# A four-layer decoder step on one core: layer norm's sum of squares by three plain additions in place of two strided sums

## The chip, the core and the metric

The kernel runs on one core of a Trainium2 chip. The metric is the device time of one execution in microseconds (us). A core has five engines that run their own instruction streams in order and wait for each other by semaphores: PE (TensorE, matrix products; its weight loads are listed as PEld), DVE (VectorE), ACT (ScalarE), POOL (GpSimd) and SP (SyncE, which here only issues DMAs).

## The reference, cut to what matters

One inference step of a decoder trunk of four layers, in float32, for a prompt of 512 positions and 8 single sample tokens: 520 columns of 1024 features. Each layer is a token mixer (sparse attention, gMLP, HGRN2, sparse attention) and a SwiGLU feed-forward block, and behind each of the eight stands a residual with a layer norm; gMLP has one more norm inside.

```python
def layer_norm(x, g, b):
    mu = jnp.mean(x, axis=-1, keepdims=True)
    var = jnp.mean(jnp.square(x - mu), axis=-1, keepdims=True)
    return (x - mu) * lax.rsqrt(var + LN_EPS) * g + b

def deepnorm(x, h, g, b):
    return layer_norm(DEEPNORM_ALPHA * x + h, g, b)
```

So nine layer norms run in a step, each over 1024 features of 520 columns.

## The kernel before, in words

Activations lie feature-major: eight blocks of 128 features, one feature a partition, and along the free axis the 520 columns, treated as two halves of 256 and 264 (`HS`, L18). A float32 matrix product is made of three products of split parts (L248 to L250), for each of the 128-row blocks k of a unit; a unit is one 128-column block of weights. After every second k, `mm` calls `tick` (L251, L252), so a tick comes after each six matmuls. A tick takes one step of every generator that has been spawned (L221 to L231): this is how work of DVE, ACT and POOL, and PE's few other products, are put between the matmuls. The instructions stand in each engine's stream in the order in which the program issues them. Weights arrive by DMA on SP's queue (L87) and are split by ACT and DVE (L100, L101) two units ahead.

`out_proj` (L364) adds the last product of a layer's block to x (L381 or L383), POOL adds up the column sums (L360, L362; the last block on DVE), and when feature block 7 of a half is there, it spawns `ln` for that half (L387). The seven last blocks run by halves: all of half 0, then all of half 1. So half 0's norm runs beside half 1's matmuls, and half 1's norm beside the first units of the next phase, which read half 0 only. gMLP spawns the same `ln` at L465.

`ln` (L263) has these steps, one a tick: three ticks of nothing (`WM`); the mean, a product of the column sums with a matrix of 1/1024 (L277, on PE); two steps that each subtract the mean from two pairs of feature blocks (L284, DVE, 512 or 528 columns) and square them (L285, ACT); two steps that each sum four squared blocks to one row (L293, DVE, a reduction that reads its 1024 or 1056 elements with the block index innermost); then the variance, the product of the two rows with the same matrix (L298, on PE, two products into one PSUM bank); the inverse root (Ln and Exp on ACT, L339 and L341; a Newton step on DVE, L348 to L352); and the scaling and split by pairs (L306 to L317, L271). `WV`, the ticks ahead of the variance, is 0. The float32 products L277 and L298 appear in the trace as two matmul records each.

With `direct` (half 1 of the very last norm alone) there are no reductions: the eight squared blocks go to PE as eight products. Squared blocks lie in tiles of the large pool `g` (38 tiles), the summed rows in the pool `row` (8 tiles).

The lines that the change touches:

```python
            nc.scalar.activation(sq[-1][:, 2 * (j % 2):2 * (j % 2) + 2], xs, AF.Square)
            if j % 2:
                yield
        for j in range(2):
            if direct:
                q += [sq[j][:, i] for i in range(4)]
            else:
                q.append(self.row()[:, :n])
                nc.vector.tensor_reduce(q[-1], sq[j].rearrange("p b t -> p t b"), op=OP.add, axis=AX.X)
            yield
        yield from wait(WV)
        pv = self.ps()
        for i, r in enumerate(q):
            nc.tensor.matmul(pv[:, :n], self.ones, r, start=i == 0, stop=i == len(q) - 1)
```

Of the kernel before, what the change touches and what calls it, by code (L numbers as in the profile page):

```python
# [11 lines left out]
OP = mybir.AluOpType  # L12
AX = mybir.AxisListType
# [6 lines left out]
EPS = 1e-5  # L20
CH = (8, 7, 7)
NFF = sum(CH)
SLOTS = 38        # tiles of the pool that nearly everything lives in
WM, WV = 3, 0     # layer norm: ticks before the mean's and the variance's matrix products
# HGRN: order of a head's four projections (q, forget gate, v, output gate), units that run by halves first, ticks
# before a head's levels, levels built ahead, ticks of the sample's part, rate of the last head, output units beside it
HORD, HF, HW, BUILD, SW0, SWAIT, HRATE, EARLY = (0, 1, 2, 3), 6, 1, 3, 0, 8, 2, 6
# NSA: units between scores and mix, blocks between transposes and values, steps that exp and the like are put off
LAG, PVLAG, DEFER = 2, 3, 1
# NSA: steps a tick of attention (beside W_in, beside W_out) and of compression, and of the others for one of attention  # L30
RATE, RATE2, CRATE, STEPS = 4, 4, 1, 1
# NSA: steps that the sample's pages, values and compressed rows are waited for, tokens whose pages load ahead
CWAIT, EWAIT, AHEAD = 8, 5, 5
# [8 lines left out]
def alternate(*gs):  # L42
    """Steps of some generators in turn, until all end."""
    live = list(gs)
    while live:
        for x in list(live):
            try:
                next(x)
                yield
            except StopIteration:  # L50
                live.remove(x)
# [17 lines left out]
class Weights:  # L69
    """Streams weight blocks: DMA, then a split in two float32r parts, ahead of their use."""  # L70

# [45 lines left out]
class Split:  # L117
    """Activations by blocks of features, as two float32r parts whose sum is exact."""

# [24 lines left out]
class Net:  # L144
# [67 lines left out]
    def spawn(self, g, rate=1.0):  # L212
        """A generator whose steps are issued between those of the matrix products."""
        self.par.append([g, rate, 0.0])
        return g
# [21 lines left out]
    def mm(self, unit, nk, R, half, ks=None, p=None):  # L237
        """One 128-column block of weights times the columns of a half: three passes a block of rows."""
        nc = self.nc
        H, L = self.W.need(unit)  # L240
        c0, c1 = HS[half]
        n = c1 - c0
        if p is None:
            p = self.ps()
        for k in ks or range(nk):
            s = slice(k * 128, k * 128 + 128)
            a, b = R.get(k, c0, c1)
            nc.tensor.matmul(p[:, :n], H[:, s], a, start=k == 0, stop=False)  # L248
            nc.tensor.matmul(p[:, :n], L[:, s], a, start=False, stop=False)  # L249
            nc.tensor.matmul(p[:, :n], H[:, s], b, start=False, stop=k == nk - 1)  # L250
            if k % 2:  # L251
                self.tick()  # L252
        return p

    @staticmethod
    def order(n, first, last):
        """(index, half): the first and the last few by halves, the others both halves together."""
        o = [(i, 0) for i in range(first)] + [(i, 1) for i in range(first)]
        for i in range(first, n - last):
            o += [(i, 0), (i, 1)]  # L260
        return o + [(i, 0) for i in range(n - last, n)] + [(i, 1) for i in range(n - last, n)]

    def ln(self, cols, li, sums, pair, X=None, out=None, direct=False):  # L263
        """Layer norm over the features, in place; its split goes to X, or out(j, c0, c1, pair) follows each pair.
        With direct, the tensor engine alone sums the squares."""
        nc = self.nc
# [6 lines left out]
        c0, c1 = cols  # L273
# [6 lines left out]
        for j in range(4):  # L280
# [5 lines left out]
            if j % 2:  # L286
                yield
        for j in range(2):
            if direct:
                q += [sq[j][:, i] for i in range(4)]  # L290
            else:
                q.append(self.row()[:, :n])
                nc.vector.tensor_reduce(q[-1], sq[j].rearrange("p b t -> p t b"), op=OP.add, axis=AX.X)  # L293
            yield
# [32 lines left out]
    def table(self, i):  # L327
        """The set of ScalarE's tables that the next functions need: one set for exp and ln together."""
        nc = self.nc
        if self.tab != i:  # L330
            self.tab = i
            nc.scalar.add_instruction(mybir.InstLoadActFuncSet(
                act_func_set_id=i, name=nc.get_next_instruction_name(), engine=mybir.EngineType.Activation))

    def guess(self, ys, vs):
        """y = exp(-ln(var + EPS) / 2), guesses at 1 / sqrt(var + EPS)."""
        self.table(LN_EXP)
        for y, v in zip(ys, vs):
            self.nc.scalar.activation(y, v, AF.Ln, bias=self.eps[:, 0:1])  # L339
        for y in ys:  # L340
            self.nc.scalar.activation(y, y, AF.Exp, scale=-0.5)  # L341

    def newton(self, ys, vs):
        """A Newton step from the guesses, and -2 times the results."""
        nc = self.nc
        ws = [self.row()[:, :y.shape[1]] for y in ys]
        for w, y, v in zip(ws, ys, vs):
            nc.vector.scalar_tensor_tensor(w, v, EPS, y, op0=OP.add, op1=OP.mult)  # L348
        for w, y in zip(ws, ys):
            nc.vector.tensor_mul(w, w, y)  # L350
        for w, y in zip(ws, ys):
            nc.vector.scalar_tensor_tensor(y, w, -3.0, y, op0=OP.add, op1=OP.mult)  # L352
# [11 lines left out]
    def out_proj(self, units, nk, R, scale, li, first=0, last=7, final=False, early=0):  # L364
        """x = scale * x + W h by blocks of features; with li the layer norm runs behind it."""
        nc = self.nc
# [153 lines left out]
    def bounds(self):  # L520
        """The heads' lower bounds of the forget gates, and the norm's gain."""
        nc, a = self.nc, self.a
# [23 lines left out]
    def hgrn(self, layer, plan):  # L546
# [26 lines left out]
        def sample(h, QK, FV, G, S0):  # L573
            """The sample tokens of a head: their states one step on, and what they read from them."""
            yield from wait(SW0)
# [27 lines left out]
        def head(h, QK, FV, G, smp):  # L603
# [6 lines left out]
            def build(i):  # L610
                """Queries times decays from a block's start, keys times decays to its end, by doubling blocks."""
                x, y = self.slot(), cur[i - 1]
# [22 lines left out]
            def odd(ap, i):  # L635
                """Columns in the second halves of the blocks of a level: its queries."""
                if i == 0:
                    return ap.rearrange("p c (n w) -> p c n w", n=1)
                return ap.rearrange("p c (n b w) -> p c n b w", b=2, w=2 ** (i - 1))[:, :, :, 1]
# [125 lines left out]
    def nsa(self, layer, plan):  # L765
# [49 lines left out]
        def summaries(cm, n, b):  # L815
            """Compressed keys and values of n pages; with b == 8, of the prompt, whose last page is the position term."""
            cv = cm.rearrange("p n (v l j) -> p n v l j", v=2, l=8)
# [15 lines left out]
        def compress():  # L833
            """Of the prompt first, then of each token's pages."""
            yield from wait(12)
# [46 lines left out]
        def attend():  # L882
            """Causal attention of the groups' heads over the prompt: three branches, by blocks of queries."""
            D, pv, due = {}, [], []
# [105 lines left out]
            def products(lag):  # L990
                """Values times transposed probabilities, behind the transposes."""
                while len(pv) > lag:
# [39 lines left out]
        def sample():  # L1032
            """Attention of the sample tokens, rows (token, head), over their pages, windows and new rows."""
            Qp = self.slot()[:, 0, :512].rearrange("p (v b c) -> p v b c", v=2, b=8)
# [22 lines left out]
            def rows(br, v):  # L1057
                """The keys or the values of each token's pages or window, loaded ahead."""
                ts = []
# [236 lines left out]
def constants(np):  # L1296
    """Arrays that depend on shapes alone: identity, masks, selectors."""
    p = np.arange(128)
# [12 lines left out]
def arrange(np, i):  # L1311
    """Inputs as the kernel reads them: permuted, with weights in blocks of 128 columns."""
    i = {k: np.asarray(v) for k, v in i.items()}
# [53 lines left out]
def results(r):  # L1367
    """Outputs as the reference has them."""
    y = r["yT"].transpose(2, 1, 0).reshape(T, 1024)
# [25 lines left out]
```

## Time and profile before

| what | us | share of the span |
|---|---|---|
| runs, median of 3 (lowest, highest) | 3125.0 (3124.13, 3129.43) | |
| profiled execution, span | 3127.9 | |
| PE busy | 2960.0 | 95% |
| PE weight loads busy | 2772.8 | 89% |
| DVE busy | 1734.5 | 55% |
| ACT busy | 1296.0 | 41% |
| POOL busy | 472.8 | 15% |

The profile is of one execution; its span lies within the runs' own spread, 2.9 us above their median. Busy time counts instructions as they run, so an engine can be far from busy and still be what another waits for. In a timeline row the first number is the start, the second the time from the start of the first to the end of the last of the merged instructions, and the bracket is the idle time of that engine ahead of it, with what ended it.

### The profile page before, as it was taken

To read this page: it belongs to the slowest core of one execution; us is meant where nothing else is said; L and a number is where in the kernel's file an instruction comes from. 1 tells how busy PE (TensorE), PEld (TensorE's weight loads), DVE (VectorE), ACT (ScalarE), POOL (GpSimd) and SP (SyncE) were. 2 spreads that over 40 slices of the span, in tenths; PEclk is the share of its full clock that TensorE was granted. 3 is DMA by queue.
4 is the path that set the end of the run, shared out by engine and by line. 5 is a ranking of instruction groups with operands and counts; after the bars stand their busy time and mean duration, and the time that the engine had idled before them with its cause. 6 is when DMAs were issued, how large, how long until landed. Compare 5 with 4: busy or idle time off the path is not lost. (4 is left out here: it accounts for less than half of the span.)

```text
span 3127.9 us, 56300 instructions
## 1 busy us (share of the span) xinstructions
PE 2960.0 (95%) x22730; PEld 2772.8 (89%) x22730; DVE 1734.5 (55%) x3821; ACT 1296.0 (41%) x2902; POOL 472.8 (15%) x446
## 2 busy tenths in 40 slices
PE   8898999999989999999899999999899999999997
PEld 8887468999988999998899889999888865799997
DVE  4887545333456633337777773333668866543334
ACT  4666434322345431234455443223456655332322
POOL 0222032000030300004222130000312212300002
PEclk9999999999999999999999999999999999999999
DMA  4222433223222222322222222232122143323221
GB/s 170 74 61 84 135 108 102 88 84 107 82 82 95 67 90 92 98 86 78 76 83 76 71 95 88 92 104 82 68 79 66 60 150 91 132 83 100 89 83 40
DMA packets 136039, 280.61 MB, mean 90 GB/s; under 512 B 13026, under 2 KB 76002, under 8 KB 135778
## 3 DMA queue, kind: packets, MB, share of 16 engines
q1 hardware_dynamic: 127168, 261.86, 26.6%
q10 hardware_dynamic: 7458, 10.95, 1.0%
q0 software_dynamic: 1152, 4.19, 0.5%
q8 instruction: 179, 2.93, 0.4%
q14 instruction: 82, 0.67, 0.1%
HBM read 263.69 MB, written 13.27 MB: 89 GB/s over the span
## 5 line engine op out<-in xcount | busy, mean ns | idle before, releaser
L248 PE MATMUL ps<-g 128*128 128x256 f32 (+1 forms) x6176 | 1784.2, 289 | 14.5 <-ACT g L100 13.2
L249 PE MATMUL ps<-g 128*128 128x256 f32 (+1 forms) x6176 | 1755.4, 284 | 6.8 <-DVE g L101 6.8
L250 PE MATMUL ps<-g 128*128 128x256 f32 (+1 forms) x6176 | 1757.1, 285 | 4.4 <-DVE g L271 2.7
L248 PEld LDWEIGHTS ps<-g 128*128 128x128 f32 x6176 | 1177.7, 191 | 37.9 <-ACT g L100 15.0
L249 PEld LDWEIGHTS ps<-g 128*128 128x128 f32 x6176 | 1177.3, 191 | 13.1 <-DVE g L101 8.3
L250 PEld LDWEIGHTS ps<-g 128*128 128x128 f32 x6176 | 1175.1, 190 | 6.1 <-DVE g L271 3.5
L101 DVE TENSOR_TENSOR g<-g 128x512 fp32r<-128x512 f32 (+1 forms) x708 | 468.6, 713 | 59.8 <-ACT g L100 52.5
L100 ACT CAST g<-g 128x512 fp32r<-128x512 f32 (+1 forms) x788 | 426.6, 608 | 118.9 <-DVE g L101 98.0
L419 DVE TENSOR_TENSOR row<-row,ps 128x256 f32<-128x256 f32 (+1 forms) x176 | 74.8, 425 | 515.7 <-PE ps L250 515.7
L209 ACT CAST g<-row 128x256 fp32r<-128x256 f32 (+1 forms) x192 | 78.6, 410 | 503.2 <-DVE row L419 491.6
L360 POOL TENSOR_TENSOR row<-x 128x256 f32<-128x256 f32 (+1 forms) x16 | 13.0, 812 | 1451.7 <-DVE x L383 1331.5
L418 ACT ACTIVATE row<-ps 128x256 f32<-128x256 f32 (+1 forms) x176 | 67.6, 384 | 334.3 <-PE ps L250 334.0
L951 ACT ACTIVATE g<-g,nst 128x128 f32<-128x128 f32 (+3 forms) x256 | 143.1, 559 | 109.8 <-DVE nst L949 109.3
L381 DVE SCALAR_TENSOR_TENSOR x<-x,ps 128x256 f32<-128x256 f32 (+1 forms) x128 | 52.9, 423 | 167.9 <-PE ps L250 167.8
L963 POOL TENSOR_SCALAR g<-g,nst 128x128 f32<-128x128 f32 (+3 forms) x64 | 76.5, 1195 | 442.7 <-DVE nst L956 378.7
L998 PE MATMUL ps<-g 128*128 128x512 f32 x384 | 141.4, 451 | 0.0
L949 DVE CUSTOM_DVE_ANT_0 g<-ps,ncst 128x128 f32<-128x128 f32 (+3 forms) x256 | 119.1, 482 | 39.4 <-PE ps L947 34.1
L947 PE MATMUL ps<-g 128*128 128x256 f32 (+2 forms) x512 | 123.9, 343 | 11.3 <-DVE nst L949 5.9
L985 ACT CAST g<-ps 128x512 fp32r<-128x512 f32 x160 | 91.9, 583 | 102.2 <-PE ps L982 83.2
L101 POOL TENSOR_TENSOR g<-g 128x512 fp32r<-128x512 f32 x80 | 105.0, 1333 | 172.8 <-ACT g L100 170.1
L383 DVE TENSOR_TENSOR x<-x,ps 128x256 f32<-128x256 f32 (+1 forms) x128 | 53.8, 424 | 135.5 <-PE ps L250 135.4
L210 DVE TENSOR_TENSOR g<-row,g 128x256 fp32r<-128x256 f32 (+1 forms) x192 | 81.7, 429 | 83.8 <-ACT g L209 83.8
(239 smaller groups left out, 2954.2 us busy)
## 6 DMA issues: line engine op xcount, KB each, us to landing
g<-ffn_in SPq DMA_DIRECT2D x176, 512.0 KB, 3.6
g<-ffn_out SPq DMA_DIRECT2D x64, 448.0 KB, 3.3
g<-nsa_in SPq DMA_DIRECT2D x42, 512.0 KB, 3.8
cm<-cache_cmp SPq DMA_DIRECT2D x64, 256.0 KB, 3.8
g<-cache_slc SPq DMA_DIRECT2D x128, 128.0 KB, 2.6
g<-cache_win SPq DMA_DIRECT2D x32, 512.0 KB, 6.5
g<-ffn_out SPq DMA_DIRECT2D x32, 512.0 KB, 3.5
g<-hgrn_in SPq DMA_DIRECT2D x32, 512.0 KB, 3.9
```

What stands on the lines that cost most here:

```text
L100: self.nc.scalar.copy(h[:, a:b], r[:, a:b])
L101: (self.sub[a > 0] or self.nc.vector).tensor_sub(l[:, a:b], r[:, a:b], h[:, a:b].bitcast(FT))
L209: self.nc.scalar.copy(h, src)
L210: self.nc.vector.tensor_sub(l, src, h.bitcast(FT))
L248: nc.tensor.matmul(p[:, :n], H[:, s], a, start=k == 0, stop=False)
L249: nc.tensor.matmul(p[:, :n], L[:, s], a, start=False, stop=False)
L250: nc.tensor.matmul(p[:, :n], H[:, s], b, start=False, stop=k == nk - 1)
L947: nc.tensor.matmul(p[:, :nn], q, kt[:, s, :nn], start=s == 0, stop=s == 1)
L949: nc.vector.tensor_tensor_reduce(P, p[:, :n], tri[:, 512 - n:], 1.0, 3e38, OP.add, OP.min, st[:, i:i + 1])
L951: defer(lambda P=P, i=i: (self.table(LN_EXP), nc.scalar.activation(P, P, AF.Exp, bias=st[:, i:i + 1], scale=-1.0, accum_out=st[:, 4 + i:5 ...
L985: nc.scalar.copy(PT[:, 0, :512], p)
L998: nc.tensor.matmul(o, v, PT[:, s, :512], start=start and s == 0, stop=stop and s == 1)
```

## The change

In a norm that is not `direct`, each of the two reductions goes. In their place, DVE adds the upper two blocks of a squared tile to the lower two (one plain addition of 512 or 528 columns, in place) as soon as the tile's four blocks are squared, which in the code is after the tick's `yield` and so, for the first tile, ahead of the next subtractions; then one more such addition joins the two tiles. The variance is again two products, of the two blocks that are left, which now are read from the squares' tile. The step sequence has one `yield` less. In a `direct` norm the steps are as before. All other lines of the diff are comments and docstrings.

```diff
@@ -254,15 +254,15 @@
...
@@ -285,12 +285,15 @@
             nc.scalar.activation(sq[-1][:, 2 * (j % 2):2 * (j % 2) + 2], xs, AF.Square)
             if j % 2:
                 yield
-        for j in range(2):
-            if direct:
-                q += [sq[j][:, i] for i in range(4)]
-            else:
-                q.append(self.row()[:, :n])
-                nc.vector.tensor_reduce(q[-1], sq[j].rearrange("p b t -> p t b"), op=OP.add, axis=AX.X)
+                if not direct:
+                    nc.vector.tensor_add(sq[-1][:, :2], sq[-1][:, :2], sq[-1][:, 2:])
+        if direct:
+            for t in sq:
+                q += [t[:, i] for i in range(4)]
+                yield
+        else:
+            nc.vector.tensor_add(sq[0][:, :2], sq[0][:, :2], sq[1][:, :2])
+            q = [sq[0][:, i] for i in range(2)]
             yield
         yield from wait(WV)
         pv = self.ps()
...
```

## Rows read from the trace of the kernel before

**Rows 1.** The page: the span, and each engine's busy time, share and instructions.

```profile
span 3127.9 us, 56300 instructions
...
PE 2960.0 (95%) x22730; PEld 2772.8 (89%) x22730; DVE 1734.5 (55%) x3821; ACT 1296.0 (41%) x2902; POOL 472.8 (15%) x446
```

**Rows 2.** Waits of PE over the whole span: total us, times, longest us.

```profile
PE ps L298 <- DVE row L293: 45.9, 34, 4.1
...
PE ps L250 <- DVE g L271: 2.7, 4, 0.8
```

**Rows 3.** Lines L293, L284, L285, L298: count, ns min/median/max, first and last start, forms.

```profile
L293 DVE TENSOR_REDUCE row<-g x34: 1876/1944/2036, 469.6 to 3094.7; 128x256 f32<-128x1024 f32 x18, 128x264 f32<-128x1056 f32 x16
...
L284 DVE TENSOR_TENSOR x<-x,ps x64: 678/690/703, 467.2 to 3112.0; 128x512 f32<-128x512 f32 x32, 128x528 f32<-128x528 f32 x32
...
L285 ACT ACTIVATE g<-x x64: 630/640/649, 468.0 to 3112.7; 128x512 f32<-128x512 f32 x32, 128x528 f32<-128x528 f32 x32
...
L298 PE MATMUL ps<-row,ones x68: 379/483/810, 471.7 to 3096.9; 128*128 128x256 f32 x36, 128*128 128x264 f32 x32
```

**Rows 4.** Timelines of DVE, ACT and PE in one half-0 norm, 1817 to 1825.

```profile
1818.33 2.48 DVE L284 TENSOR_TENSOR x<-x,ps 128x512 f32<-128x512 f32 x4
1820.72 3.76 DVE L293 TENSOR_REDUCE row<-g 128x256 f32<-128x1024 f32 x2
...
1819.05 2.42 ACT L285 ACTIVATE g<-x 128x512 f32<-128x512 f32 x4 [11.71 <-DVE x L284]
...
1817.69 0.59 PE L277 MATMUL ps<-row,ones 128*128 128x256 f32 x2
...
1821.52 0.28 PE L249 MATMUL ps<-g 128*128 128x264 f32 x1
1821.64 0.28 PE L250 MATMUL ps<-g 128*128 128x264 f32 x1
1822.74 0.70 PE L298 MATMUL ps<-row,ones 128*128 128x256 f32 x2 [0.82 <-DVE row L293]
1824.54 0.70 PE L298 MATMUL ps<-row,ones 128*128 128x256 f32 x2 [1.10 <-DVE row L293]
```

**Rows 5.** Timeline of DVE in a Newton step: dependent instructions, one behind the other.

```profile
475.42 0.42 DVE L348 SCALAR_TENSOR_TENSOR row<-ps,row 128x256 f32<-128x256 f32 x1 [1.72 <-ACT row L341]
475.88 0.42 DVE L350 TENSOR_TENSOR row<-row 128x256 f32<-128x256 f32 x1
```

**Rows 6.** Timelines of DVE and PE in a half-0 norm after a feed-forward block, 1431 to 1439.

```profile
1431.76 2.48 DVE L284 TENSOR_TENSOR x<-x,ps 128x512 f32<-128x512 f32 x4 [0.73 <-PE ps L277]
1434.15 0.42 DVE L383 TENSOR_TENSOR x<-x,ps 128x264 f32<-128x264 f32 x1
1434.49 3.75 DVE L293 TENSOR_REDUCE row<-g 128x256 f32<-128x1024 f32 x2
...
1438.30 0.70 PE L298 MATMUL ps<-row,ones 128*128 128x256 f32 x2 [1.10 <-DVE row L293]
```

**Rows 7.** Timelines of DVE and PE in a half-1 norm, 1843 to 1851.

```profile
1843.94 2.54 DVE L284 TENSOR_TENSOR x<-x,ps 128x528 f32<-128x528 f32 x4
...
1850.34 0.71 PE L298 MATMUL ps<-row,ones 128*128 128x264 f32 x2 [1.13 <-DVE row L293]
```

**Rows 8.** Timelines of DVE and PE in a half-1 norm, 2238 to 2247.

```profile
2238.88 2.54 DVE L284 TENSOR_TENSOR x<-x,ps 128x528 f32<-128x528 f32 x4
...
2243.36 1.25 PE L298 MATMUL ps<-row,ones 128*128 128x264 f32 x2 [4.09 <-DVE row L293]
2245.20 1.25 PE L298 MATMUL ps<-row,ones 128*128 128x264 f32 x2 [0.60 <-DVE row L293]
```

**Rows 9.** Stretches: us, busy (count) of PE, PEld, DVE, ACT, POOL, granted clock, DMA.

```profile
473.70:477.10 3.40, 3.40 (x16) 3.24 (x16) 1.58 (x4) 0.89 (x2) 0.74 (x1) 0.50 0.71 236
477.10:480.50 3.40, 3.40 (x30) 3.40 (x30) 2.13 (x5) 2.08 (x4) 2.27 (x4) 1.00 0.47 131
...
2726.50:2733.30 6.80, 6.03 (x24) 5.08 (x24) 4.69 (x8) 3.86 (x7) 0.00 (x0) 0.50 0.24 80
```

## The prediction, made before the changed kernel was run

> **What bounds the kernel now.** I read the page first: PE is busy for 95% of the span, DVE for 55% and ACT for 41% [rows 1]. PE takes its instructions in order, so time is won or lost where PE stands still, and DVE's busy time as such is worth nothing. The next view is that of PE's own waits [rows 2]. The largest by far is the variance product L298 waiting for the reductions L293: 45.9 us in 34 waits. The tail of a norm costs PE almost nothing: its wait for the split L271 sums to 2.7 us. So what a norm costs is the stretch from its mean to its variance. The third view is that of the lines [rows 3]: 34 reductions, two in each of 17 halves of norms (the 18th half is direct), 1.94 us each; a subtraction of as many columns as a new addition takes 0.69 us, a square 0.64 us. The last view is the timelines of single halves, where the sum is made.
>
> **What is removed.** 34 reductions, 34 x 1.94 = 66 us of DVE. **What is added.** 17 x 3 = 51 plain additions; I price each at 0.69 us, from the subtractions, which differ only in that one operand lies in PSUM: 35 us. DVE is relieved of 31 us, and I cost that at nothing, since what hides it is PE's stream; the only PE waits that end on DVE here are those of L298, and these depend on when the last sum is ready, not on DVE's total. Those queued behind the sums (an evacuation, the next weights' split) start some 0.2 us sooner; PE waits for none of them near a norm. 34 tiles of pool row fewer and squares' tiles held until the variance is read I also cost at nothing: PE reads them at the step where the rows were read. The new additions need no wait on another engine but the one for ACT's squares.
>
> **The path in one half** [rows 4]. The four subtractions start 0.60 us apart (2.48 less 0.69, by three), the second at 1818.93, and each square starts 0.03 us behind its subtraction. Before, subtractions and reductions run back to back on DVE, the reductions end at 1824.48, and the two variance products start at 1822.74 and 1824.54, each on its own row. After the change:
> - The first addition stands in DVE's queue ahead of the third subtraction and waits for the second square: subtraction to 1819.62, square from 1819.65 to 1820.29, addition from 1820.32. DVE would have been free at 1819.53, so 0.79 us are lost there, and behind the waiting addition stand the other two subtractions.
> - Third subtraction at 1820.92, fourth at 1821.52 to 1822.21, its square to 1822.88, second addition 1822.91 to 1823.60.
> - The third addition needs the second's result. Dependent instructions on DVE follow at their length and 0.04 us more [rows 5]: 1823.64 to 1824.33. The first variance product starts 0.06 us behind, as now: 1824.39, which is 5.46 us after the second subtraction.
>
> So the last sum is ready only 0.15 us sooner than now: three additions save 1.7 us of DVE work, but 0.79 us go to the wait for the second square, and the last square is reached late, with two additions still behind it. The first product can't go ahead of the second any more either. A product that follows a wait takes 0.32 us between its two records (0.70 less 0.38), one in flow some 0.22 us (0.59 less 0.38). Its last record therefore stands at 1824.39 + 0.32 + 0.22 + 0.22 = 1825.15, against 1824.54 + 0.32 = 1824.86: 0.29 us later.
>
> **The missing step.** A yield less puts the variance one tick earlier in PE's stream: 24 matmuls cover the wait, not 30. Matmuls start 0.12 us apart [rows 4], so 0.72 us of work is moved from ahead of the wait to behind it. PE arrives at 1821.2, not 1821.92, and stands until 1824.39: 3.2 us in one piece in place of 0.82 + 1.10. This half loses 0.29 + 0.72 = **1.0 us**.
>
> **The same for the others**, always with 5.46 us from the second subtraction to the first product:
> - Five halves 0 like this one: 1.0 us each, 5.0.
> - Four halves 0 after a feed-forward block, where an evacuation of 0.42 us stands between subtractions and reductions [rows 6]. After the change it falls into DVE's wait for the fourth square. Second subtraction 1432.36, product 1437.82 against 1438.30: last record 0.04 us sooner, loss 0.7 each, 2.8.
> - Three halves 1 whose products run at full clock [rows 7]: 1844.55 + 5.46 = 1850.01 against 1850.34, last record 0.1 us later, loss 0.8 each, 2.4.
> - Five halves 1 whose products run at a granted clock of 0.5 [rows 8]: there a pair's records stand about 0.6 us apart, and in flow 0.44. 2239.49 + 5.46 = 2244.95 against 2245.20, last record 0.6 us later, loss 1.4 each, 7.0. (gMLP's second half is among them; ACT is busier there, its own loss lies between 1.0 and 1.8.)
>
> Sum: **17 us** lost. Bounds: if dependent additions follow without a gap and each takes 0.1 us less, 0.4 us a half go, 7 in all; if additions take 0.1 us more beside POOL's work, 5 are added. 10 to 22.
>
> **The clock.** After a wait in a norm the granted clock was 0.5 (1.2 GHz in place of 2.4) in nine of the 17 halves, the first and the last of them in [rows 9]: 16 matmuls in 3.4 us where the next stretch has 30. A short fall thus costs 14 x 0.12 = 1.7 us. Eight halves have no fall now; six of them wait for some 1.9 us, in two pieces. With one piece of 2.8 us or more I take it that three of the eight fall: **5 us**. Bounds: four short falls of now vanish (-7), all eight fall (+14). The Trainium skill, "TensorE: Matmul & The Clock Gate", section "HAM oscillation", says that idle gaps throttle the array and that the matmuls behind them run at half clock; the trace agrees [rows 9], and the rule speaks against this change, as the third rival has it.
>
> By another page the sum would be worse still: "VectorE: DVE Perf Modes", section "The perf-mode tier table", of the Trainium skill, has reductions at one element a cycle, by which (an estimate with the page's 0.96 GHz and 151 cycles) 1024 elements take 1.22 us; were that so, two removed reductions would pay 1.4 us less in each half, and the loss would be about 41 us. The rows have 1.94 us, and the sum goes by them.
>
> **Sum against the profiled execution**: 3127.9 + 17 + 5 = 3150 us of span. The median of the runs is 2.9 us lower, so 3125.0 + 22 = **3147 us**.
>
> **Rivals.**
> 1. Not slower but faster: DVE isn't held at the first addition. The point is the order on DVE: were the subtractions 3 and 4 to run ahead of it, the last sum would be ready 1.4 us sooner (0.79 of wait and 0.60 of the addition's place), each half would gain 0.4 us in place of losing 1.0, 17 x 0.4 = 7 us: 3118. For it: the saved 31 us of DVE are real. Against: DVE runs in the code's order in every timeline (L383 stays between L284 and L293 [rows 6]), and the code has the addition first. Chance 0.08.
> 2. No change: the moved six matmuls and the late products fall into idle time that PE has behind the norm anyway; the sum shrinks to the clock's scatter: 3125, give or take 6. For it: PE idles for 168 us of the span [rows 1]. Against: behind L298 PE is in flow, and its wait for the norm's end is 2.7 us in all [rows 2]. Chance 0.12.
> 3. Slower by more: the single, longer wait lowers the clock in all eight halves that keep it now, and in some longer: 17 + 14 and some 7 more for four longer falls, 3163. Chance 0.1, since of the halves that wait for 1.9 us some fall now and most don't. [...]
>
> **How the numbers follow.** The forecast has 0.7. A measurement of this kernel can tell about 0.2%, 6 us, from no change. The bounds of the forecast give 3125 + 10 - 7 = 3128 to 3125 + 22 + 14 = 3161; the range is stretched to 3126 and 3164 to hold part of the second and of the third rival, and leaves out the first. Faster 0.08; same 0.13 (the second rival and the forecast's edge); slower 0.79.
>
> **What would show it.** In the new profile, PE's waits at L298 should come to about 67 us in 17 or so waits, in place of 45.9 in 34: 3.2 us in the half of [rows 4] and over 5 us in that of [rows 8]. DVE should be 31 us less busy, with a gap of 0.8 us ahead of the first addition and one of 0.7 us ahead of the second, in all 17 halves; the first product should stand 5.46 us behind the second subtraction. The granted clock should be 0.5 behind about twelve norms, not nine. The forecast is wrong if DVE's gap ahead of the first addition is missing, if additions take well under 0.6 us, if PE's total wait there falls under 46 us, or if PE makes up the lost time elsewhere.

## The result, and the profile after

| | before | changed |
|---|---|---|
| median of 5 runs, us | 3125.1 | 3153.9 |
| lowest to highest, us | 3124.1 to 3129.4 | 3152.1 to 3158.0 |
| profiled span, us | 3127.9 | 3150.4 |

The changed kernel is slower by 28.8 us, a ratio of 1.009 with a 95% interval of 1.0078 to 1.0102. The forecast was 3147, the range 3126 to 3164.

The page of the changed kernel (span; busy time, share and instructions of each engine), beside [rows 1]:

```profile
span 3150.4 us, 56325 instructions
...
PE 2964.8 (94%) x22730; PEld 2782.6 (88%) x22730; DVE 1715.0 (54%) x3838; ACT 1296.2 (41%) x2902; POOL 463.3 (15%) x446
```

PE has the same 22730 instructions. DVE has 17 more (51 added, 34 removed) and is 20 us less busy, and the span is longer all the same. PE's waits in the changed kernel (total us, times, longest us), beside [rows 2]; the variance product is now L301, the third addition L295:

```profile
PE ps L301 <- DVE g L295: 67.8, 17, 7.2
...
PE ps L248 <- ACT g L100: 13.3, 4, 10.7
```

The wait at the variance went from 45.9 us in 34 pieces to 67.8 us in 17: one piece a half. The wait for the norm's tail, L250 for L271, 2.7 us before, is no longer in the list. The lines of the additions (count, ns min/median/max, and what their engine sat idle for), beside [rows 3]:

```profile
L289 DVE TENSOR_TENSOR g<-g x34: 692/708/1074, 462.9 to 3115.0; 128x512 f32<-128x512 f32 x18, 128x528 f32<-128x528 f32 x16
...
  ACT g L285: 24.1, 34
...
L295 DVE TENSOR_TENSOR g<-g x17: 691/693/1120, 466.2 to 3116.2; 128x512 f32<-128x512 f32 x9, 128x528 f32<-128x528 f32 x8
```

An addition takes the 0.69 to 0.71 us that it was priced at, and up to 1.1. All 34 of the first two additions of a norm make DVE stand still for ACT's squares, 24.1 us in all, 0.7 on average. Now the half of [rows 4], timelines of DVE, ACT and PE in the changed kernel:

```profile
1830.00 1.29 DVE L284 TENSOR_TENSOR x<-x,ps 128x512 f32<-128x512 f32 x2
1831.98 0.69 DVE L289 TENSOR_TENSOR g<-g 128x512 f32<-128x512 f32 x1 [0.70 <-ACT g L285]
1832.59 1.28 DVE L284 TENSOR_TENSOR x<-x,ps 128x512 f32<-128x512 f32 x2
1834.57 0.69 DVE L289 TENSOR_TENSOR g<-g 128x512 f32<-128x512 f32 x1 [0.69 <-ACT g L285]
1835.29 0.69 DVE L295 TENSOR_TENSOR g<-g 128x512 f32<-128x512 f32 x1
...
1830.72 1.23 ACT L285 ACTIVATE g<-x 128x512 f32<-128x512 f32 x2 [11.79 <-DVE x L284]
1833.31 1.23 ACT L285 ACTIVATE g<-x 128x512 f32<-128x512 f32 x2 [1.35 <-DVE x L284]
...
1832.59 0.28 PE L250 MATMUL ps<-g 128*128 128x264 f32 x1
1836.04 1.32 PE L301 MATMUL ps<-g,ones 128*128 128x256 f32 x4 [3.16 <-DVE g L295]
1836.82 0.76 PE L248 MATMUL ps<-g 128*128 128x264 f32 x1
```

The four subtractions that ran back to back are torn into two pairs with an addition and a gap between them, and ACT, too, now stands still for 1.35 us between its pairs of squares. The second subtraction starts at 1830.60, the product at 1836.04: 5.44 us. PE stands for 3.16 us in one piece, not 0.82 + 1.10.

In the halves 0 after a feed-forward block [rows 6] the third addition ends later than the prediction had it. Timelines of DVE and POOL in the changed kernel:

```profile
865.12 0.42 DVE L386 TENSOR_TENSOR x<-x,ps 128x264 f32<-128x264 f32 x1
865.89 1.07 DVE L289 TENSOR_TENSOR g<-g 128x512 f32<-128x512 f32 x1 [0.36 <-ACT g L285]
867.00 0.69 DVE L295 TENSOR_TENSOR g<-g 128x512 f32<-128x512 f32 x1
...
865.68 0.74 POOL L365 TENSOR_TENSOR row<-row,x 128x264 f32<-128x264 f32 x1 [4.21 <-DVE x L386]
```

The evacuation (L386 here) does fall into the wait, as said, but POOL's addition to the column sums then runs beside the second addition, which takes 1.07 us: 5.82 us from subtraction to product in these four halves.

The granted clock (eighth column of the stretches) behind a half 0 and a half 1 of the changed kernel, beside [rows 9]:

```profile
468.10:471.50 3.40, 3.40 (x18) 3.40 (x17) 2.35 (x5) 1.23 (x3) 0.00 (x0) 0.50 0.80 284
...
2256.80:2267.00 10.20, 5.24 (x20) 4.83 (x21) 6.66 (x13) 5.52 (x10) 0.00 (x0) 0.50 0.12 47
```

Below, such a stretch at 0.50 is called a fall of the clock. Read in this way, 16 of the 17 halves have a fall behind or in their wait; nine had before.

**Where the time came from.** PE's matmuls at L248 to L250 are the same 18528 in the same order in both kernels, so each can be set beside its twin. From the one ahead of the mean to the one some 19 us behind it, a half lost 0.88 to 1.05 us in the six halves where the clock did as before, and 2.4 to 2.7 us in six where a short fall is new. The two groups differ by 1.6 us. The other five lost 1.6 to 3.8; in three of them the clock was at 0.50 for longer than before. Over all halves that is some 34 us, of which 5 came back between the norms. One thing disturbs the two profiles' comparison: before the first norm, the profiled execution of before spent a stretch of its attention at half clock, which the changed one didn't. The stretch, in the kernel before:

```profile
374.70:384.90 10.20, 10.20 (x28) 4.99 (x28) 6.25 (x20) 4.15 (x11) 1.89 (x2) 0.50 0.40 117
```

Its first norm begins at 466.46, that of the changed kernel at 460.18. From there to the end the kernels take 2661.4 and 2690.2 us: 28.8 us more, the difference of the medians.

### The profile page after: what moved, and what is told of

Its sections match the earlier page's. It is cut to its first block, busy times and chain, and to the rows that moved or that the text cites. A ratio compares the mean times of both kernels' runs of the same rounds, so it can differ in the third digit from the quotient of the medians.

```text
span 3150.4 us, 56325 instructions
## 1 busy us (share of the span) xinstructions
PE 2964.8 (94%) x22730; PEld 2782.6 (88%) x22730; DVE 1715.0 (54%) x3838; ACT 1296.2 (41%) x2902; POOL 463.3 (15%) x446
## 5 line engine op out<-in xcount | busy, mean ns | idle before, releaser
L248 PE MATMUL ps<-g 128*128 128x256 f32 (+1 forms) x6176 | 1790.0, 290 | 14.4 <-ACT g L100 13.3
L250 PE MATMUL ps<-g 128*128 128x256 f32 (+1 forms) x6176 | 1759.5, 285 | 1.7 <-DVE g L210 1.7
L248 PEld LDWEIGHTS ps<-g 128*128 128x128 f32 x6176 | 1181.8, 191 | 38.0 <-ACT g L100 14.9
L250 PEld LDWEIGHTS ps<-g 128*128 128x128 f32 x6176 | 1178.5, 191 | 2.5 <-DVE g L210 2.5
L100 ACT CAST g<-g 128x512 fp32r<-128x512 f32 (+1 forms) x788 | 426.7, 608 | 119.0 <-DVE g L101 98.1
L386 DVE TENSOR_TENSOR x<-x,ps 128x256 f32<-128x256 f32 (+1 forms) x128 | 53.8, 424 | 146.7 <-PE ps L250 146.7
```

The costliest lines, as they stand in the source:

```text
L100: self.nc.scalar.copy(h[:, a:b], r[:, a:b])
```

## The experiments

Each is timed against the kernel before on its chip, whose medians there were 3124.6 to 3125.4 us. A difference is to the kernel named.

**e1: the step put back.**

```diff
             q = [sq[0][:, i] for i in range(2)]
             yield
+            yield
```

> The changed kernel with the missing step put back: one more yield between the third addition and the variance products, so 30 matmuls cover the wait again and not 24. Theory (a step is worth six matmuls of 0.12 us): each of 17 halves stands 0.72 us less at L301, the sum of that wait goes from 67.8 to about 56 us, and some 3 of the 16 falls of the clock in norms go, 1.6 us each: 3153.9 - 12 - 5 = 3137 us (3134 to 3142). Rival A (only the late additions count, the step doesn't): 3154. Rival B (the clock alone makes the loss, and it falls as often): 3142 at the least, with 16 falls as now.

Measured: 3131.2 us (3127.9 to 3137.1; ratio 1.0017, 1.0007 to 1.0027), 22.7 us less than changed and below the range that was expected. PE's wait:

```profile
PE ps L302 <- DVE g L295: 56.6, 17, 5.8
```

The wait is 11.2 us shorter, as expected. Still 15 of 17 halves have a fall of the clock, but the stretches in and behind norms at 0.50 add up to 61 us, not 85: there are short falls where there were long ones. So one step of six matmuls is worth 23 us here. About half of it is wait; 24 us less at half speed make some 12 us, an estimate that fits the other half. This sets rival A aside, and the time lies below rival B's least, too.

**e2: the first addition behind the subtractions.**

```diff
-                if not direct:
-                    nc.vector.tensor_add(sq[-1][:, :2], sq[-1][:, :2], sq[-1][:, 2:])
...
         else:
+            for t in sq:
+                nc.vector.tensor_add(t[:, :2], t[:, :2], t[:, 2:])
             nc.vector.tensor_add(sq[0][:, :2], sq[0][:, :2], sq[1][:, :2])
```

> The changed kernel with the first addition moved behind the last two subtractions; nothing else, the step still missing. Theory (the first addition, waiting for the second square, holds the subtractions back by 0.79 us and its own place of 0.60): the first product stands some 4.05 us behind the second subtraction and not 5.5, the wait at L301 falls from 67.8 to about 44 us, and some falls of the clock go: 3153.9 - 24 - 7 = 3123 us (3118 to 3130). Rival A (what costs is the three additions' own time and their chain, wherever they stand): 3154. Rival B (the missing step is all of it): 3154.

Measured: 3125.5 us (3122.1 to 3129.7; ratio 1.0001, 0.9991 to 1.0010), 28.4 us less than changed. DVE's timeline in the half of [rows 4], and PE's waits:

```profile
1819.53 2.48 DVE L284 TENSOR_TENSOR x<-x,ps 128x512 f32<-128x512 f32 x4
1821.93 1.47 DVE L294 TENSOR_TENSOR g<-g 128x512 f32<-128x512 f32 x2
1823.44 0.69 DVE L295 TENSOR_TENSOR g<-g 128x512 f32<-128x512 f32 x1
```

```profile
PE ps L301 <- DVE g L295: 46.6, 17, 5.8
PE ps L248 <- ACT g L100: 20.4, 6, 10.9
```

The same three additions run almost without a gap, and the product follows the second subtraction by 4.04 us. The wait is 21 us shorter, not 24, since the evacuation now stands ahead of the additions in the four halves of [rows 6] (4.75 us there). Eight of 17 halves still have a fall. A part is lost to 7 us more of waiting for the split of the next weights (L248 for L100, 13.3 us in the changed kernel).

**e12: the first addition between the last two subtractions.**

```diff
+            if j == 2 and not direct:
+                nc.vector.tensor_add(sq[0][:, :2], sq[0][:, :2], sq[0][:, 2:])
             if j % 2:
                 yield
-                if not direct:
-                    nc.vector.tensor_add(sq[-1][:, :2], sq[-1][:, :2], sq[-1][:, 2:])
+                if not direct and j == 3:
+                    nc.vector.tensor_add(sq[1][:, :2], sq[1][:, :2], sq[1][:, 2:])
```

> The changed kernel with the first addition behind the third subtraction, not ahead of it; steps as changed. It tells the first addition's wait for the second square (0.79 us) from its place on DVE (0.60): here 0.18 of the wait are left and the whole place. Theory: the first product stands 4.8 us behind the second subtraction, between 5.44 (changed) and 4.05 (e2); the wait at the variance falls from 67.8 to about 57 us: 3154 - 10.5 - 4 for falls of the clock = 3139 us. Rival A (the place alone costs): 3154. Rival B (the wait alone costs): 3127, near e2.

Measured: 3145.6 us (3139.3 to 3150.0; ratio 1.0068, 1.0050 to 1.0087), 8.3 us less than changed. DVE's timeline in the half of [rows 4], and PE's wait:

```profile
1824.08 1.88 DVE L284 TENSOR_TENSOR x<-x,ps 128x512 f32<-128x512 f32 x3
1826.06 0.69 DVE L287 TENSOR_TENSOR g<-g 128x512 f32<-128x512 f32 x1
1826.67 0.68 DVE L284 TENSOR_TENSOR x<-x,ps 128x512 f32<-128x512 f32 x1
1828.05 0.69 DVE L291 TENSOR_TENSOR g<-g 128x512 f32<-128x512 f32 x1 [0.69 <-ACT g L285]
```

```profile
PE ps L303 <- DVE g L297: 59.1, 17, 6.6
```

The product stands 4.84 us behind the second subtraction, as expected between 5.44 and 4.04: 0.6 us go with most of the wait for the second square, 0.8 with the rest of that wait and the addition's place. The wait is 8.7 us shorter. The median is above the forecast of 3139; its four runs lie within 11 us, and in the profiled one, the lowest, 13 halves still have a fall.

**e3 and e4: the kernel before, with a step less and with a step more.**

```diff
                 nc.vector.tensor_reduce(q[-1], sq[j].rearrange("p b t -> p t b"), op=OP.add, axis=AX.X)
-            yield
+            if direct or j:
+                yield
```

```diff
         yield from wait(WV)
+        yield from wait(0 if direct else 1)
```

> The kernel before, both reductions kept, with both in one step: one yield less, 24 matmuls ahead of the variance. Theory: each half stands 0.72 us more at L298, 45.9 to about 58 us, with two or three more falls of the clock: 3125 + 12 + 4 = 3141 us (3136 to 3146). Rival (the additions make the loss, the step nothing): 3125.

> The kernel before, both reductions kept, with one more step ahead of the variance (36 matmuls cover the wait). Theory: each half stands 0.72 us less, 45.9 to about 34 us, and a few of the nine falls go: 3125 - 12 - 4 = 3109 us (3104 to 3114). Rival (PE's stream is full, a matmul moved ahead of the wait is only moved): 3125.

Measured: e3 3145.4 us (3142.6 to 3150.5; ratio 1.0069, 1.0051 to 1.0087), with this wait of PE:

```profile
PE ps L299 <- DVE row L293: 56.0, 34, 5.5
```

So the step alone, with not one addition in the kernel, costs 20 us of the 29. The waits of a half are still two pieces here (1.5 and 1.1 us in most halves 0), and 15 of 17 halves have a fall: here the clock fell more often with longer waits, in two pieces too. e4: 3127.3 us (3122.3 to 3133.8; ratio 1.0007, 0.9997 to 1.0017), a miss. Its waits of PE:

```profile
PE ps L299 <- DVE row L293: 36.3, 28, 3.0
...
PE ps L250 <- DVE g L271: 11.9, 14, 1.2
```

The wait at the variance did shrink by 10 us, but the same 9 us appear as the wait for the norm's tail, which the added step puts later: the matmul that first reads the half's low parts is there ahead of them. The rival named (a matmul is only moved) isn't what happened; a second wait that was just covered came out.

**e5: both undone, plain additions kept.** e2's edit and e1's.

> Three additions behind the subtractions as in e2, and the missing step put back as in e1: what the plain additions are worth against the reductions at the same number of steps. Theory (place and step are separate costs and add up): 3125.5 - 12 of waits (46.6 to about 35 us at the variance) - 4 for falls of the clock = 3109 us (3103 to 3115); the wait for the norm's tail at L250 stays small, as the sums are ready 1.4 us sooner. Rival (the longer sequence makes the norm's tail late, as in e4): 3125 with a wait of some 10 us at L250 for the split.

Measured: 3104.6 us (3104.3 to 3111.1; ratio 0.9942, 0.9925 to 0.9958). PE's waits:

```profile
PE ps L302 <- DVE g L295: 36.8, 17, 4.7
...
PE ps L250 <- DVE g L271: 3.4, 5, 0.9
```

As in the kernel before, 30 matmuls cover the wait. The tail's wait stays at 3.4 us: the variance isn't a step later than before, as it is in e4, and the additions are done sooner.

**e7: the first addition issued a step earlier, straight behind the fourth subtraction.**

```diff
             if j % 2:
+                if not direct and j == 3:
+                    nc.vector.tensor_add(sq[0][:, :2], sq[0][:, :2], sq[0][:, 2:])
                 yield
-                if not direct:
-                    nc.vector.tensor_add(sq[-1][:, :2], sq[-1][:, :2], sq[-1][:, 2:])
+                if not direct and j == 3:
+                    nc.vector.tensor_add(sq[1][:, :2], sq[1][:, :2], sq[1][:, 2:])
...
             yield
+            yield
```

> As e5, but the first addition is issued straight behind the fourth subtraction, a step earlier and so ahead of the evacuation that stands there in halves 0 after a feed-forward block. Theory: the first product stands 4.05 us behind the second subtraction in those four halves too, not 4.75, others as in e5: 3 us less than e5. Rival (the evacuation behind the addition then comes late and holds up a matmul): e5 or slower.

Measured: **3102.0 us** (3101.3 to 3104.3; ratio 0.9929, 0.9912 to 0.9945), the fastest version of all, 23 us under the kernel before. The intervals of e5 and e7 overlap, so the 2.5 us between them aren't shown; the four halves of [rows 6] have 4.62 us to the product in place of 4.76, not the 4.05 expected: the evacuation now stands ahead of the second addition, and the third takes 1.11 us beside POOL's addition. Timeline of DVE and PE in the half of [rows 4]:

```profile
1800.38 2.48 DVE L284 TENSOR_TENSOR x<-x,ps 128x512 f32<-128x512 f32 x4
1802.78 0.68 DVE L288 TENSOR_TENSOR g<-g 128x512 f32<-128x512 f32 x1
1803.56 0.69 DVE L291 TENSOR_TENSOR g<-g 128x512 f32<-128x512 f32 x1
1804.29 0.69 DVE L297 TENSOR_TENSOR g<-g 128x512 f32<-128x512 f32 x1
...
1805.04 1.13 PE L304 MATMUL ps<-g,ones 128*128 128x256 f32 x4 [1.04 <-DVE g L297]
```

**e9: the changed kernel, with PE fed in the wait.** The added products' output is overwritten and used by nothing.

```diff
         pv = self.ps()
+        if not direct:
+            for i in range(8):
+                nc.tensor.matmul(pv[:, :128], self.ones, self.ones, start=True, stop=True)
```

> The changed kernel with eight matrix products of 128 columns ahead of the two of the variance, into the same bank, which the variance then overwrites (work that the output doesn't use): PE does them while it waits for the third addition, so the wait is filled in part and the path isn't longer. Theory (each short fall of the clock behind a norm costs 1.6 us): of 16 falls in norms few are left, 3154 - 16 x 1.6 = 3128 us, or 3135 if a third of them stays. Rival A (the clock is beside the point, the wait for the sum is all): 3154. Rival B (the added products push the rest of PE's stream): 3154 + 17 x 1 = 3171.

Measured: 3143.0 us (3141.9 to 3145.9; ratio 1.0061, 1.0044 to 1.0078), 10.9 us less than changed, with more work. PE's timeline and the clock behind it in the half of [rows 4], and PE's waits:

```profile
1828.80 1.84 PE L302 MATMUL ps<-ones 128*128 128x128 f32 x15
1832.02 1.13 PE L304 MATMUL ps<-g,ones 128*128 128x256 f32 x4 [1.38 <-DVE g L295]
...
1832.50:1835.90 3.40, 3.40 (x29) 3.32 (x28) 1.65 (x4) 0.89 (x2) 0.69 (x1) 1.00 0.01 2
...
PE ps L304 <- DVE g L295: 38.8, 17, 5.4
PE ps L248 <- ACT g L100: 19.2, 7, 10.6
```

The product starts 5.44 us behind the second subtraction, as in the changed kernel, so the path is the same. But five of 17 halves have a fall left, not 16, and in the seven halves 0 whose short fall went, 1.5 to 1.6 us came back each. In the half 0 that had no fall, the same edit changed the time by less than 0.1 us. So this is the price of a short fall. The total misses the 3128 to 3135 us of the theory: three halves 1 now wait some 2 us each for the next weights' split (13.3 to 19.2 us in all), and stretches at half clock outside the norms were 90 us in this execution, against 66 in that of the changed kernel.

**e10 and e11: e7 with more cover in half 1 alone**, by a step (`yield from wait(c0 > 0)` behind e7's last `yield`) or by e9's eight products.

> e7 with one more step ahead of the variance in half 1 alone, where the wait is still 2 to 4.7 us. Theory: 8 halves x 0.72 = 6 us of waits go and one or two falls of the clock: 3102 - 8 = 3094 us. Rival (as in e4, the tail is late or the next weights' split takes the wait's place): 3102, with the wait at L248 for L100 or at L250 for L271 up by some 6 us.

> e7 with eight unused matrix products of 128 columns ahead of the variance in half 1 alone, to keep PE at work in the wait; no step is added. Theory (a fall of the clock costs 1.6 us and the products fit into the wait): the six falls left go in part, 3102 - 4 x 1.6 = 3096 us. Rival (halves 1 wait for the next weights' split anyway): 3102.

Measured: e10 3113.4 us (3112.9 to 3113.7; ratio 0.9961, 0.9947 to 0.9975), e11 3106.7 us (3101.5 to 3107.7; ratio 0.9934, 0.9917 to 0.9950). Neither beats e7, and e10 is slower. PE's waits in e10:

```profile
PE ps L305 <- DVE g L297: 29.6, 17, 4.0
...
PE ps L250 <- DVE g L271: 11.1, 16, 1.2
```

The step in half 1 takes 6 us off one wait (35.4 in e7) and puts 8 on the tail's (2.8 in e7), the rival of the expectation, as in e4. These two waits make 2 us of the 11 that e10 is slower than e7. Its stretches at 0.50 add up to 120 us, those of e7 to 97, and the growth lies outside the norms; at half speed that is some 12 us, an estimate. Why the clock fell more there isn't shown. In e11 the wait at the variance fell to 21.6 us and the time didn't follow; this isn't explained either.

## Why the prediction was right or wrong

Medians by where the sums stand and how many matmuls cover the wait (27, 33 and 42 in four of the halves):

| sums | 24 matmuls | 30 | 36 |
|---|---|---|---|
| two reductions | 3145.4 (e3) | 3125.1 (before) | 3127.3 (e4) |
| additions, first one ahead | 3153.9 (changed) | 3131.2 (e1) | |
| additions, all behind | 3125.5 (e2) | 3104.6 (e5) | |

- **What bounds**: right. DVE is 20 us less busy, and this was worth nothing by itself. It was to be 31: the additions took 37.6 us and not 35, the norms' later multiplications 5 us more, and instructions that now stand apart no longer overlap a little at their ends.
- **The path**: right. 5.44 us from second subtraction to product against 5.46 in the half of [rows 4]. The prediction took 5.46 for all halves, which was too short for many: 5.55 us in most halves 1, which have more columns, 5.82 in the halves of [rows 6], and 7.18 in gMLP's second half, where ACT does other work ahead of the squares. Three additions give 20 us when they don't stand in the subtractions' way (e5 against before), and cost 6 us when they do (e1 against before). e12 splits the difference into wait and place.
- **The missing step**: right in its direct part, 11.2 us of wait in e1 against 12. Its whole worth is 20 to 23 us (the first two columns of each row of the table), since PE's longer wait also lowers the clock. The sum had both, but booked the clock apart.
- **Waits**: 67.8 us in 17, against "about 67 in 17 or so".
- **The halves**: 0.88 to 1.05 us where the clock is as before; the sum had 1.0 for the halves 0 of [rows 4], but 1.4 for halves 1 at half clock, which was too much, and 0.7 for the halves of [rows 6], whose product came 0.36 us later than it had, beside POOL's addition.
- **The clock**: mis-sized. The sum had three new falls, 5 us; seven came (16 of 17 halves, not 12), and some old ones grew. The price, 1.7 us, was right within 0.2 (e9). Seven at 1.6 make 11 us, 6 more than booked. Of the 34 us lost in the halves, some 6 more are left for the longer falls, which the sum put at nothing, and 5 came back between the norms. Together these are the 7 us that the forecast is short. So the forecast's nearness is in part errors that cancel. The third rival had the mechanism at its full size, 3163, and the time lies between the two. The Trainium skill's page "TensorE: Matmul & The Clock Gate", section "HAM oscillation", describes idle gaps of PE behind which the matmuls run at half clock; the runs agree in this, with a fall in 16 of 17 halves. In e9, PE fed with unused products kept its clock at 1.00 behind the wait of [rows 4], over the same path.
- **The profiled execution**: the sum of 3150 met its span of 3150.4, in part by luck: the execution of before was one of its slower ones (the stretch at half clock ahead of the first norm), and that of the changed kernel its fastest.
- **The rivals**: the first (not held at the first addition) falls by the timeline. Its order is that of e2, and even that is no faster than before, since the step is missing. The second (made good behind the norm) holds for 5 of 34 us.
- The prediction costed the tail of a norm at almost nothing, from 2.7 us of waiting. e4 and e10 show how near it stands: one step more ahead of the variance brought out 8 to 9 us of waiting there.

What stays open: why a wait of 3.2 us lowered the clock in one half and not in another of the same length (gMLP's first half in the changed kernel has none), why the clock fell more outside the norms in e10, why e11 gained nothing, and what part of the scatter of some runs (10 us in e12) are falls elsewhere.

## What to carry to other kernels

An instruction that waits for another engine holds what stands behind it on its engine, as the first addition did here (0.7 us of waiting): put the combining work behind the producers (e2's edit, -28 us), and count the place as well as the wait. In a kernel whose work is dealt out in steps, a step removed is cover removed: price it in PE's work, and again for the clock, which here fell in more places when PE's waits grew. Before cover is added, look which wait is just covered behind it, since that one comes out next.

## What was not expected of the hardware

- Two waits of PE of about 1 us with a pair of products between them lowered the granted clock in 3 of 9 halves 0; one wait of 3.2 us did in 8 of 9, and in e3 two waits of 1.5 and 1.1 us did in 7 of 9. In e2, waits of 1.8 to 2.0 us in one piece did so in none of seven halves, waits of 2.1 us in four of four. But two of its halves 1 waited 3.2 us, and no fall came for 12 us behind the product, so the length of the wait alone doesn't decide.
- A plain addition on DVE beside POOL's addition to a row took 1.07 to 1.12 us, not 0.69 to 0.71, in all five places of the changed kernel where the two met.
- The strided reduction of 1024 elements took 1.94 us, against 0.69 us for an addition of 512: two reductions, 3.9 us, and three additions, 2.1 us, leave PE the same two products.
